# Attention with an added bias on one core: scores kept in PSUM across heads, and more exponentials on VectorE

## The chip, the core and the metric

The kernel runs on one core of a Trainium2 chip. The core has engines that run side by side and are ordered by semaphores: TensorE (PE in the profile; PEld is its loading of weights), VectorE (DVE), ScalarE (ACT) and GpSimd (POOL). The queues of SyncE (SP), ACT and POOL start transfers; those of POOL can convert f32 to bf16 on the way. Matmuls write into PSUM, a memory of eight banks of 512 f32 values for each of 128 partitions. SBUF is the larger memory that everything else lives in. The metric is the time of one execution on the device in microseconds, the median of several.

## The reference

For 4 batches with 8 heads each, a sequence of 1024 and a head dimension of 64, attention with a bias that all heads share:

```python
scores = scale * np.matmul(q, k.transpose(0, 1, 3, 2))   # scale = 1/8
scores = scores + bias                                    # (1, 1, 1024, 1024)
attn = np.exp(scores - scores_max) / (np.sum(np.exp(scores - scores_max), axis=-1, keepdims=True) + 1e-8)
return np.matmul(attn, v)
```

All inputs are f32, drawn with a standard deviation of 0.1. The kernel leaves out the subtraction of the maximum, since the scores are small, and gets the sum of a row's exponentials from a column of ones beside V.

## The kernel before

The 32 heads are taken as 16 pairs (`NP`). Scores are made transposed, keys on partitions and queries along the row, so that the exponentials can be the weights of the second product as they are. A *bank* is the unit of the scores: 128 keys (chunk `kc` of 8) by 512 queries (half `qh` of 2) of one head, one PSUM bank. There are 512 banks.

**Loads and transposes.** POOL loads K and Q of a pair with conversion to bf16 (`load_qk`, L75 to L80), three pairs ahead, and V two pairs ahead into `vall` (`load_v`, L82). TensorE transposes K and Q (`transpose_pe`, L86) into one of two single PSUM banks `xa` and `xb`; VectorE copies them out. K of both heads lies stacked on the partitions (head 0 on 0 to 63, head 1 on 64 to 127). Q is copied twice with a mask that zeroes the other head's half (L102), so that one matmul over 128 partitions gives the scores of one head.

**Scores and exponentials.** `s_fill` (L165) makes three banks with three matmuls of 512 columns (L172) in one of two PSUM tiles of three banks each (`ps_s`); `s_exp` (L178, L180) lets ScalarE exponentiate the three banks in one instruction into `E` in SBUF, as bf16. While ScalarE reads one tile, TensorE can fill the other.

**The bias.** For most banks exp(S + bias) is made as exp(S) times exp(bias): in the beginning the bias is transposed (`b_fill`, L220) and exponentiated once (`b_exp`, L230, L232) into `eb`, and VectorE multiplies every pair of banks by it (`mul_pair`, L235, two banks on L245 and L239, four on L242). For 64 banks (the chunks `kc` 6 and 7 of the second half of the queries) the bias is added in PSUM by one more matmul of 512 columns (L176, L193), and no product follows.

**Exponentials on VectorE.** Six of those 64 banks are never seen by ScalarE. VectorE turns the scores into fixed point (L201) and makes 2^x from integer and fraction with a polynomial in six further steps over two banks at a time (`d_steps`, L205, lines L212 to L217): two scalar operations and four that combine two operands.

**Second product.** `av_bank` (L261) multiplies the exponentials of a bank with V and the ones column, four matmuls of 65 columns each with its own weights (L269), summed over the chunks in `xa` or `xb`. The evacuation takes the reciprocal of the sum (L279), multiplies (L281), and SP's queue stores the result.

**The order of the work.** It is written out ahead by a planner (from L412): it keeps a clock for ScalarE, VectorE and TensorE, books each instruction with a fixed cost, and lets the engine that can start first emit its next one. TensorE prefers the fill of the next score tile (`pe_fill`, L470), and in the time that it is not needed takes a transpose (`pe_piece`, L496), a fill for VectorE's exponentials (`pe_d`, L553) or a product (`pe_av`, L635). VectorE takes what is ready first, by rank (`dve_pick`, L688). The engines then run these lists in order; only waits decide the actual times. The start (L324 to L410) is written by hand: the first half of the first pair is loaded by SP and ACT as f32, converted on VectorE and ScalarE, and dummy matmuls keep TensorE busy until then.

Of the kernel before, what the change touches and what calls it, by code (L numbers as in the profile page):

```python
# [16 lines left out]
def kernel(  # L17
# [11 lines left out]

# [7 lines left out]
    HQ = S // 2  # L40
    QC = NCH // 2
# [3 lines left out]
    vf = v.rearrange("b (g t) (p c) d -> (b g) p t c d", t=2, p=P)  # L45
    of = out.rearrange("b h (p c) d -> (b h) p c d", p=P)
    bf_ = bias.rearrange("a b (p c) k -> p (a b c) k", p=P)

    consts = ctx.enter_context(tc.tile_pool(name="consts", bufs=1))
    raw = ctx.enter_context(tc.tile_pool(name="raw", bufs=3))  # L50
    kvp = ctx.enter_context(tc.tile_pool(name="kvp", bufs=3))
    ep = ctx.enter_context(tc.tile_pool(name="ep", bufs=6))
    op = ctx.enter_context(tc.tile_pool(name="op", bufs=2))
    dp = ctx.enter_context(tc.tile_pool(name="dp", bufs=1))
    de = ctx.enter_context(tc.tile_pool(name="de", bufs=2))
    small = ctx.enter_context(tc.tile_pool(name="small", bufs=4))
    ps_s = ctx.enter_context(tc.tile_pool(name="ps_s", bufs=2, space=bass.MemoryType.PSUM))
    ps_x = ctx.enter_context(tc.tile_pool(name="ps_x", bufs=1, space=bass.MemoryType.PSUM))

    ident = consts.tile([P, P], BF)  # L60
    warm = consts.tile([P, 1], F32)
    btraw = consts.tile([P, NCH, S], BF)
    eb = consts.tile([P, 2, NCH, HQ], BF)
    braw = consts.tile([P, 2, HQ], BF)
    mask = consts.tile([P, 2, HQ], BF)
    vall = consts.tile([P, 2 * NP, NCH, D1], BF)

    k0f = consts.tile([P, 2, QC, D], F32)
    q0f = [consts.tile([P, QC, D], F32, name=f"q0f{t}") for t in range(2)]
    zeros = consts.tile([P, P], BF)  # L70

    raws = {}
    trs = {}

    def load_qk(pr):  # L75
        qr = raw.tile([P, 2, NCH, D], BF, name="qr")
        kr = raw.tile([P, 2, NCH, D], BF, name="kr")
        nc.gpsimd.dma_start(out=kr.rearrange("p t c d -> p t (c d)"), in_=kf[pr])  # L78
        nc.gpsimd.dma_start(out=qr.rearrange("p t c d -> p t (c d)"), in_=qf[pr])  # L79
        raws[pr] = (qr, kr)  # L80

    def load_v(pr):  # L82
        for t in range(2):
            nc.gpsimd.dma_start(out=vall[:, 2 * pr + t, :, :D], in_=vf[pr, :, t])  # L84

    def transpose_pe(pr, which, c0, n, tag):  # L86

        src = raws[pr][which]
        px = ps_x.tile([P, n, P], BF, tag=tag, name="px")
        for c in range(n):  # L90
            for t in range(2):
                nc.tensor.transpose(px[t * D:(t + 1) * D, c, :], src[:, t, c0 + c, :], ident[:])  # L92
        if (pr, which) not in trs:
            trs[(pr, which)] = (kvp.tile([P, NCH, P], BF, name="kT") if which else
                                kvp.tile([P, 2, NCH * P], BF, name="qT"))
        dst = trs[(pr, which)]

        def copy():
            if which == 0:

                m = n // QC
                nc.vector.tensor_tensor(  # L102
                    dst[:, :, c0 * P:(c0 + n) * P].rearrange("p t (m q) -> p t m q", m=m),
                    px.rearrange("p (m c) q -> p m (c q)", m=m).unsqueeze(1).to_broadcast([P, 2, m, HQ]),
                    mask.unsqueeze(2).to_broadcast([P, 2, m, HQ]), op=ALU.mult)
            else:
                nc.vector.tensor_copy(dst[:, c0:c0 + n, :], px[:])  # L107
        return copy


    NE = NCH - 2
    DPR = (3, 7, 11)
    banks = [(0, h, 0, kc) for kc in range(NCH) for h in range(2)]

    def mix(early, late, singles):
        while early or late:
            if late and (singles(len(banks), len(early) + len(late)) or not early):
                banks.append(late.pop(0))
            else:
                banks.extend(early[:2])  # L120
                del early[:2]

    for pr in range(NP):
        early = [(pr, h, 1, kc) for kc in range(NE) for h in range(2)]
        late = [(pr, h, 1, kc) for kc in range(NE, NCH - (pr in DPR)) for h in range(2)]
        if pr == NP - 1:
            early = [(pr, h, 1, kc) for h in range(2) for kc in range(NE)]
            late = [(pr, h, 1, kc) for h in range(2) for kc in range(NE, NCH)]
        if pr == 0:
            early += [(1, h, 0, kc) for kc in range(NCH) for h in range(2)]  # L130
            mix(early, late, lambda b, left: b % 3 == 2 and b > 36)
        else:
            if pr > 1:
                banks += [(pr, h, 0, kc) for kc in range(NCH) for h in range(2)]
            mix(early, late, lambda b, left: b % 3 == 2 and (pr < NP - 1 or left > 8))
    NB = len(banks)

    dgroups = []
    for pr in DPR:
        dgroups.append((pr, [len(banks), len(banks) + 1]))  # L140
        banks += [(pr, h, 1, NCH - 1) for h in range(2)]
# [5 lines left out]
    for b in range(len(banks)):  # L147
        units.setdefault(banks[b][:3], []).append(b)
# [112 lines left out]
    def av_bank(b, tag):  # L261
# [9 lines left out]
        if not last:  # L271
            return None
# [522 lines left out]
```

## Time and profile before

Three runs gave 246.46, 246.47 and 246.8 us; the median is 246.47 us.

| What | before |
|---|---|
| profiled execution (span) | 246.5 us |
| ACT busy | 236.7 us, 96%, 181 instructions |
| PE busy | 229.9 us, 93%, 3154 matmuls |
| DVE busy | 219.2 us, 89%, 366 instructions |
| POOL busy | 55.3 us, 22% |
| exponentials of scores (L180) | 170 instructions, 227.9 us |
| exp(bias) (L232) | 4 instructions, 6.7 us |
| products with exp(bias) (L242, L245) | 158 instructions, 136.4 us |
| matmuls for the scores (L172) | 454 in the trace, 134.9 us |
| DMA | 23.80 MB moved, mean 97 GB/s |

How to read it: the busy time of an engine is the time in which at least one of its instructions runs. Instructions in a row overlap in part, so the time of one (its mean in ns) can be longer than the distance from one start to the next; where many follow each other, the distance counts. For matmuls the ends are modelled, so that PE looks busier than it is. In the line of slices each digit is the busy share, in tenths, of one fortieth of the span. In the groups, "idle before" is the time for which the engine sat idle ahead of these instructions and what it waited for. A few matmul records are missing from the trace (454 of the 506 matmuls of L172 are in it).

### The profile page before, as it was taken

Reading aid. Unit: us, or ns where it says so; the run is one execution under the profiler, and the core shown is the slowest. Engines: PE = TensorE matmul, PEld = TensorE weight load, DVE = VectorE, ACT = ScalarE, POOL = GpSimd, SP = SyncE. Lnnn points to the kernel's source line nnn. Section 1 sums busy time; section 2 is a strip of 40 time slices with the busy share of each in tenths; the row PEclk is TensorE's granted clock in tenths of the full one; section 3 lists DMA queues with packets and bytes.
Section 4 is the critical chain, followed back from the end, with each engine's and each line's share of the span. In section 5 each row is a group of like instructions: output and inputs, shape, how many; then the busy total and the mean of one; then the engine's idle time right before and its main releaser. Section 6 shows DMA issues by size and latency. Waiting matters only on the chain.

```text
span 246.5 us, 7234 instructions
## 1 busy us (share of the span) xinstructions
PE 229.9 (93%) x3154; PEld 144.8 (59%) x3207; DVE 219.2 (89%) x366; ACT 236.7 (96%) x181; POOL 55.3 (22%) x76
## 2 busy tenths in 40 slices
PE   8667999999999999999988999999998999999993
PEld 3244656665566656666654665666664566766653
DVE  2417799998999999999999999999999999999994
ACT  5599999999999999999999999999999999999993
POOL 7654333501441304140134000601500000000000
PEclk9799999999999999999999999999999999999999
DMA  5999995995689479492394920792911020202022
GB/s 113 179 197 193 192 131 102 148 84 122 65 123 160 51 122 121 107 116 80 56 127 91 82 88 25 114 122 75 140 45 45 1 88 4 86 1 88 35 77 65
DMA packets 48752, 23.80 MB, mean 97 GB/s; under 512 B 34512, under 2 KB 44624, under 8 KB 48720
## 3 DMA queue, kind: packets, MB, share of 16 engines
q0 software_dynamic: 42560, 14.42, 53.6%
q1 hardware_dynamic: 5872, 8.72, 9.8%
q8 instruction: 25, 0.41, 0.7%
q10 hardware_dynamic: 288, 0.20, 0.3%
q14 instruction: 7, 0.06, 0.1%
HBM read 29.36 MB, written 8.39 MB: 153 GB/s over the span
## 4 chain that ended last, share of the span: by engine, by line
ACT 45%; PE 44%; DVE 4%; DMA 2%; issue 2%; POOL 1%; ACTq 0%; POOLq 0%
ACT E L180 42%; PE ps L172 24%; PE po L269 13%; PE px L92 3%; PE ps L176 3%; ACT eb L232 3%; DMA kr<-in_k_dram 2%; DVE qT L102 1%; DVE E L242 1%; DVE E L239 1%; PE pd L192 1%; PE pd L193 1%; DVE oall L281 1%; DVE db L215 0%; DVE dy L201 0%
## 5 line engine op out<-in xcount | busy, mean ns | idle before, releaser
L180 ACT ACTIVATE E<-ps 128x1536 bf16<-128x1536 f32 (+1 forms) x170 | 227.9, 1525 | 2.8 <-PE ps L172 2.7
L172 PE MATMUL ps<-qT,kT 128*128 128x512 bf16 x454 | 134.9, 382 | 8.2 <-ACT E L180 3.3
L269 PEld LDWEIGHTS <-E 128*128 128x128 bf16 x1992 | 78.9, 98 | 34.1 <-DVE E L242 2.5
L269 PE MATMUL po<-vall,E 128*128 128x65 bf16 x1992 | 84.8, 194 | 0.8 <-DVE E L245 0.3
L242 DVE TENSOR_TENSOR E<-E,eb 128x2048 bf16<-128x2048 bf16 x60 | 72.4, 1217 | 0.0
L245 DVE TENSOR_TENSOR E<-E,eb 128x1024 bf16<-128x1024 bf16 x98 | 64.0, 683 | 4.2 <-ACT eb L232 4.0
L172 PEld LDWEIGHTS <-kT 128*128 128x128 bf16 x506 | 44.9, 97 | 36.6 <-issue 10.2
L84 POOL DMA_DIRECT2D vall<-in_v_dram x32 | 28.7, 902 | 7.1 <-DMA btraw<-in_bias_dram 3.5
L281 DVE TENSOR_TENSOR oall<-po,rs 128x256 f32<-128x256 f32 x63 | 26.7, 425 | 2.2
L78 POOL DMA_DIRECT2D kr<-in_k_dram x15 | 10.5, 699 | 64.5 <-PE px L92 62.4
L102 DVE TENSOR_TENSOR qT<-px,mask 128x2048 bf16<-128x2048 bf16 (+1 forms) x17 | 19.2, 1127 | 5.6 <-PE px L92 5.4
L79 POOL DMA_DIRECT2D qr<-in_q_dram x15 | 10.7, 716 | 48.2 <-PE px L92 47.2
L176 PE MATMUL ps<-braw,ident 128*128 128x512 bf16 x57 | 21.4, 378 | 0.1
L279 DVE RECIPROCAL rs<-po 128x4 f32<-128x4 f32 x63 | 11.2, 178 | 3.3 <-PE po L269 2.5
L107 DVE COPY kT<-px 128x1024 bf16<-128x1024 bf16 (+1 forms) x16 | 10.4, 652 | 0.8 <-PE px L92 0.8
L92 PEld LDWEIGHTS <-qr 128*64 128x64 bf16 x248 | 7.5, 109 | 5.4 <-issue 5.1
L92 PEld LDWEIGHTS <-kr 128*64 128x64 bf16 x240 | 7.2, 109 | 5.0 <-issue 4.7
L92 PE MATMUL px<-ident,qr 128*64 128x128 bf16 x248 | 10.2, 222 | 0.0
L92 PE MATMUL px<-ident,kr 128*64 128x128 bf16 x240 | 9.7, 222 | 0.0
L176 PEld LDWEIGHTS <-ident 128*128 128x128 bf16 x58 | 5.6, 97 | 6.9
L232 ACT ACTIVATE eb<-pb 128x2048 bf16<-128x2048 bf16 (+1 forms) x4 | 6.7, 1676 | 0.0
L226 PEld LDWEIGHTS <-btraw 128*128 128x128 bf16 x56 | 4.0, 146 | 2.0 <-issue 1.6
(59 smaller groups left out, 65.7 us busy)
## 6 DMA issues: line engine op xcount, KB each, us to landing
out_dram<-oall SPq DMA_DIRECT2D x28, 256.0 KB, 2.0
vall<-in_v_dram POOLq DMA_DIRECT2D x32, 128.0 KB, 5.5
kr<-in_k_dram POOLq DMA_DIRECT2D x15, 256.0 KB, 4.3
qr<-in_q_dram POOLq DMA_DIRECT2D x15, 256.0 KB, 4.7
btraw<-in_bias_dram POOLq DMA_DIRECT2D x4, 512.0 KB, 8.7
out_dram<-oall SPq DMA_DIRECT2D x7, 128.0 KB, 1.8
k0f<-in_k_dram SPq DMA_DIRECT2D x2, 128.0 KB, 3.0
q0f<-in_q_dram ACTq DMA_DIRECT2D x1, 128.0 KB, 2.6
```

The lines of the kernel that those rows point to most:

```text
L84: nc.gpsimd.dma_start(out=vall[:, 2 * pr + t, :, :D], in_=vf[pr, :, t])
L92: nc.tensor.transpose(px[t * D:(t + 1) * D, c, :], src[:, t, c0 + c, :], ident[:])
L102: nc.vector.tensor_tensor(dst[:, :, c0 * P:(c0 + n) * P].rearrange("p t (m q) -> p t m q", m=m), px.rearrange("p (m c) q -> p m (c q)", m= ...
L172: nc.tensor.matmul(ps[:, j, :], kT[:, kc, :], qT[:, h, qh * HQ:(qh + 1) * HQ], start=True, stop=b not in late_bias)
L176: nc.tensor.matmul(ps[:, j, :], ident[:], braw[:, late_bias[b], :], start=False, stop=True)
L180: nc.scalar.activation(e_at(slots[g][0], n), open_ps.pop(("S", g))[:, :n, :], ACTF.Exp, scale=scale)
L232: nc.scalar.activation(eb[:, qh, :n, c0 * P:(c0 + 2) * P], open_ps.pop(("B", qh, c0))[:, :n].rearrange("p k c q -> p k (c q)"), ACTF.Exp)
L242: nc.vector.tensor_tensor(e, e, eb[:, qh, kc:kc + 2, :].unsqueeze(2).to_broadcast([P, 2, 2, HQ]), op=ALU.mult)
L245: nc.vector.tensor_tensor(e, e, eb[:, qh, kc:kc + 1, :].to_broadcast([P, n, HQ]), op=ALU.mult)
L269: nc.tensor.matmul(acc[:, i, :], e[:, 0, i * P:(i + 1) * P], vall[:, 2 * pr + h, kc, :], start=(first and i == 0), stop=last, skip_group_c ...
L279: nc.vector.reciprocal(rs[:], acc[:, :, D:D1])
L281: nc.vector.tensor_tensor(oall[:, c0:c0 + QC, :], acc[:, :, :D], rs[:].to_broadcast([P, QC, D]), op=ALU.mult)
```

## The change

The change rewrites how the scores are made and ordered.

*Running scores.* The queries are split into three passes of chunks of 128: A takes chunks 6 and 7, B 3 to 5, C 0 to 2. Six PSUM banks, `XY`, two tiles of three, hold the scores plus the bias for one pass, the even half-step in one and the odd in the other (pass A uses two banks of each). At the start of a pass (a *restart*) the bias is transposed into PSUM by matmuls of 128 columns, with the bias as weights and 8 times the identity moving, and the first head's scores are added. For each further head the tile is not made anew: one matmul over 128 partitions adds this head's scores and takes away the last head's. For head 1 of a pair the operands are `KA` (both heads stacked) and `QA` (the first half negated); for head 0 they are `KB` and `QB`, in which the second half belongs to the pair before. ScalarE's exp reads the tile and leaves it as it is. The order is: pairs 0 and 1 in the passes A, B, C; pairs 2 to 7 in C, B, A; pairs 8 to 15 in A, B, C. That makes 96 steps (a pass, a pair, a head) of two half-steps, and seven restarts.

*No exp(bias).* `eb`, `mul_pair`, the mask and the separate handling of the late chunks go.

*Operands.* K and Q of up to nine pairs are kept. VectorE copies K out of PSUM, copies Q out with a sign for each partition, and makes -Q in SBUF. Since `KB` and `QB` have halves of neighbouring pairs, four copies from SBUF to SBUF for each pair go through SP's queue. V is loaded in one DMA for a pair into a dense tile, and VectorE copies it beside the ones column.

*VectorE's exponentials.* Chunks of two banks (the last bank of both half-steps of a head 0) are marked while the order is planned, whenever VectorE's booked load is under a bound and fewer than two chunks are open; 40 banks come out. Their scores are read from the running tile in PSUM (`d_fixed`), so the tile's next fill waits for this as well as for the exp. The six further steps use the same scratch for all chunks.

*Products.* A unit is a pair in a pass: both heads are summed in one PSUM bank (`xa` or `xb`), and evacuated and stored together. The products are taken in the order of the units; within a unit, whichever bank is ready first. E is one ring of 44 banks.

*Start.* The first exp needs K of head 0, chunks 6 and 7 of Q and column chunk 6 of the bias, all loaded as f32 by SP and ACT and converted; the rest of the bias comes on POOL's queue.

```diff
-                m = n // QC
-                nc.vector.tensor_tensor(
-                    dst[:, :, c0 * P:(c0 + n) * P].rearrange("p t (m q) -> p t m q", m=m),
-                    px.rearrange("p (m c) q -> p m (c q)", m=m).unsqueeze(1).to_broadcast([P, 2, m, HQ]),
-                    mask.unsqueeze(2).to_broadcast([P, 2, m, HQ]), op=ALU.mult)
...
+    def v_copy(pr):
+        nc.vector.tensor_copy(VV[:, pr % RP, :, :D], vst.pop(pr)[:])
...
+    def k_out(pr, px):
+        nc.vector.tensor_copy(KA[:, pr % RP, :], px.rearrange("p c q -> p (c q)"))
+        if pr > 1:
+            nc.sync.dma_start(out=KB[:D, pr % RP, :], in_=KA[:D, pr % RP, :])
+        if pr + 1 < NP:
+            nc.sync.dma_start(out=KB[D:, (pr + 1) % RP, :], in_=KA[D:, pr % RP, :])
+
+    def q_out(pr, px):
+        nc.vector.tensor_scalar(QA[:, pr % RP, :], px.rearrange("p c q -> p (c q)"), sgn[:, :1], None, op0=ALU.mult)
+
+    def q_neg(pr, c0=0):
+        qn = qnp.tile([P, NCH * P], BF, name="qn")
+        nc.vector.tensor_scalar(qn[:], QA[:, pr % RP, :], -1.0, None, op0=ALU.mult)
+        nc.sync.dma_start(out=QB[:D, pr % RP, c0:], in_=qn[:D, c0:])
+        if pr + 1 < NP:
+            nc.sync.dma_start(out=QB[D:, (pr + 1) % RP, :], in_=qn[D:, :])
...
+        if restart:
...
+                    nc.tensor.matmul(ps_[:, cc:cc + P],
+                                     btraw[:, c + j, :].rearrange("p (kp kc) -> p kc kp", kc=NCH)[:, kc, :],
+                                     ident8[:], start=cc // 512 not in seen, stop=False, skip_group_check=True)
...
+        for kc, c, n, col in pcs:
+            kcol, qcol = slice(kc * P, (kc + 1) * P), slice(c * P, (c + n) * P)
+            o = ps_[:, col:col + n * P]
+            if restart:
+                lhsT, rhs = KA[:D, r, kcol], QB[:D, r, qcol]
+            elif h == 1:
+                lhsT, rhs = KA[:, r, kcol], QA[:, r, qcol]
             else:
...
+                lhsT, rhs = KB[:, r, kcol], QB[:, r, qcol]
+            nc.tensor.matmul(o, lhsT, rhs, start=False, stop=True, skip_group_check=True)
...
+    def s_exp(s, n, pos):
+        e_pos[s] = pos
+        nc.scalar.activation(E[:, pos * 512:(pos + n) * 512], XY[s % 2][:, :n * 512], ACTF.Exp, scale=scale)
...
+    def d_fixed(ch, j, s, b):
+        y = ys[ch % 2].bitcast(I32)
+        nc.vector.tensor_scalar(y[:, j * 512:(j + 1) * 512], XY[s % 2][:, b * 512:(b + 1) * 512],
+                                scale * LOG2E * 65536.0, 127.0 * 65536.0, op0=ALU.mult, op1=ALU.add)
...
+            (690, lambda: v_.tensor_scalar(sf, lo, G / 65536.0, None, op0=ALU.mult)),
+            (690, lambda: v_.tensor_scalar(sp, hi, 0.0, 128.0, op0=ALU.max, op1=ALU.mult)),
+            (1217, lambda: v_.scalar_tensor_tensor(y, sf, U1, sf, op0=ALU.add, op1=ALU.mult)),
+            (1217, lambda: v_.scalar_tensor_tensor(sb, sf, U2, sf, op0=ALU.add, op1=ALU.mult)),
+            (1217, lambda: v_.scalar_tensor_tensor(sb, sb, V2, sp.bitcast(BF), op0=ALU.add, op1=ALU.mult)),
+            (1217, lambda: v_.scalar_tensor_tensor(e[:], y, V1, sb, op0=ALU.add, op1=ALU.mult)),
...
-    def mul_pair(b, n=2):
...
+        nc.vector.reciprocal(rs[:], acc[:, :, :, D:D1])
+        nc.vector.tensor_tensor(ob[:], acc[:, :, :, :D], rs[:].to_broadcast([P, 2, W, D]), op=ALU.mult)
+        nc.sync.dma_start(out=of[pr][:, :, c0 * D:(c0 + W) * D], in_=ob.rearrange("p t c d -> p t (c d)"))
...
+        nc.sync.dma_start(out=k0f[:, :NCH * D], in_=kf[0][:, 0])
+        nc.scalar.dma_start(out=c6f, in_=bf_[:, 6, :])
+        nc.sync.dma_start(out=q0f.rearrange("p (t x) -> p t x", t=2), in_=qf[0][:, :, 6 * D:])
+        nc.sync.dma_start(out=k0f[:, NCH * D:], in_=kf[0][:, 1])
+        nc.scalar.dma_start(out=c7f, in_=bf_[:, 7, :])
...
+        load_qk(1)
+        nc.gpsimd.dma_start(out=qr0[:, :, :6, :].rearrange("p t c d -> p t (c d)"), in_=qf[0][:, :, :6 * D])
+        load_v(0)
+        nc.gpsimd.dma_start(out=btraw[:, 3:6, :], in_=bf_[:, 3:6, :])
+        load_v(1)
+        nc.gpsimd.dma_start(out=btraw[:, :3, :], in_=bf_[:, :3, :])
+        load_qk(2)
...
+            ready = max(act_end[s - 2], fix_end.get(s - 2, 0), o) + SEM
...
+                if h == 0 and s % 2 == 0:
+                    if d_load - t < DLIM and len(open_ch) < 2 and s >= DMIN and s < NS - DTAIL:
...
+                        d_load = max(d_load, t) + 7800
...
+        DLIM, DMIN, DTAIL, DMAL, RING, PSL, URG = 3500, 8, 10, 2600, 12, 180, 6
```

## Prediction

> **What bounds the kernel now.** I read the profile's page first (busy shares, slices), then the groups of instructions with their shapes apart, then the waits, then the timeline of single engines. The profiled execution takes 246.5 us, the median of the runs shown is 246.47 us, so the sum can be made against the span.
>
> The page's busy shares and its forty slices:
>
> ```profile
> PE 229.9 (93%) x3154; PEld 144.8 (59%) x3207; DVE 219.2 (89%) x366; ACT 236.7 (96%) x181; POOL 55.3 (22%) x76
> ...
> ACT  5599999999999999999999999999999999999993
> ```
>
> ACT is at 9 from the third slice to the last but one. From 9.71 us (first full exp) to 241.73 us (end of the last) the stage view gives it 232.02 us busy of 232.02. The waits say the same: of the few times that ACT waited for a matmul, nearly all is one wait of 2.6 us in the start.
>
> ```profile
> ACT E L180 <- PE ps L172: 2.7, 2, 2.6
> PE ps L172 <- ACT E L180: 3.3, 10, 0.5
> ```
>
> So the time is 9.7 us of start + 232.0 us of ScalarE + 4.8 us of tail. VectorE and TensorE have little room, but nothing of theirs ends last. The durations I need, from the groups by shape (mean ns is a single instruction's latency):
>
> ```profile
> L180 ACT ACTIVATE E<-ps 128x1536 bf16<-128x1536 f32 x167 | 225.4, 1536 | 2.6 <-PE ps L172 2.6
> L232 ACT ACTIVATE eb<-pb 128x2048 bf16<-128x2048 bf16 x2 | 3.8, 1890 | 0.0
> L281 DVE TENSOR_TENSOR oall<-po,rs 128x256 f32<-128x256 f32 x63 | 26.7, 425 | 2.2
> L107 DVE COPY kT<-px 128x1024 bf16<-128x1024 bf16 x14 | 9.6, 685 | 0.0
> L201 DVE TENSOR_SCALAR dy<-pd 128x512 int32<-128x512 f32 x6 | 4.1, 686 | 0.7 <-PE pd L193 0.6
> L217 DVE SCALAR_TENSOR_TENSOR de<-dy,db 128x1024 bf16<-128x1024 f32 x3 | 3.7, 1219 | 0.0
> L212 DVE TENSOR_SCALAR df<-dy 128x1024 f32<-128x1024 uint16 x3 | 2.1, 685 | 0.0
> ```
>
> What a row costs in a full stream is the distance between starts. The chain has the large activations one after the other: 1.34 to 1.35 us for three banks, 1.77 us for 2048 elements. Two sizes give 0.06 us + 0.427 us per 512 elements. VectorE's timeline gives its steps: independent instructions start 0.60 us apart where one lasts 0.68, while a multiply that needs the reciprocal starts 0.03 us after that has ended.
>
> ```profile
> 103.03 0.68 DVE L245 TENSOR_TENSOR E<-E,eb 128x1024 bf16<-128x1024 bf16 x1
> 103.69 0.18 DVE L279 RECIPROCAL rs<-po 128x4 f32<-128x4 f32 x1
> 103.90 0.42 DVE L281 TENSOR_TENSOR oall<-po,rs 128x256 f32<-128x256 f32 x1
> 104.25 1.28 DVE L245 TENSOR_TENSOR E<-E,eb 128x1024 bf16<-128x1024 bf16 x2
> ```
>
> **ScalarE.** The change splits the 512 banks of scores into 64 half-steps of two banks (pass A) and 128 of three (B, C), and 40 of the banks go to VectorE. Instructions: 64 x 0.916 + 128 x 1.343 - 40 x 0.427 = 58.6 + 171.9 - 17.1 = 213.4 us. Before, by the same rule: 167 x 1.343 + 0.9 + 6.2 for the four exp(bias) = 231.4. ScalarE loses 18 us; what follows decides how much of that is kept.
>
> **Start.** Before, ACT streams from 9.71 us with three banks (1.3 us) already done. Now the first exp needs half of pair 0's K (256 KB), a column of the bias (512 KB), a bit of Q (128 KB), a cast (L212's 0.69) and 24 matmuls of 128 columns. The old start's 128 KB loads took 3.0 us to land; the page's slices move 113 to 197 GB/s. The 0.9 MB needed, with the 0.77 MB queued beside it, lands between 5 us (only its own bytes, twice 190 GB/s since cast loads read two bytes for each one counted) and 10 us (all of it at 190). With cast and matmuls (x6 of 512 took 2.74 us just then, half speed) the first exp lies between 7.5 and 13 us. I take 9.9, the middle of the landing. Pass B needs a bias of 1.5 MB on POOL's queue behind K, Q and V of two pairs, by 17.2 us (9.9 + 8 x 0.916); with all ahead of it that is 5.1 MB read, 3.4 MB written. At twice 190 GB/s of reading it is there at 15, at the page's written bytes (0.7 MB in the first slice of 6.2 us, 1.1 in each later one) at 21: a loss of 0 to 4 us, 2 taken.
>
> **VectorE.** It loses the 98 + 60 multiplies by exp(bias) (136 us of rows) and the masked Q copies (19), and gets:
> - 20 chunks of two banks: two L201, L212 and L213 at 0.68, four like L217. All overlapped: 4 x 0.60 + 4 x 1.13 = 6.9 us; all dependent (each duration + 0.03): 7.8. Most steps here read their predecessor, so 7.45: 149 us.
> - 48 evacuations of both heads: reciprocal 0.21 and a multiply of 384 or 256 (by L281 and L217 about 1.03 ns an element: 557 or 425 long, 0.47 or 0.34 apart): 32 x 0.69 + 16 x 0.55 = 31.
> - per pair a K and a Q copy out of PSUM like L107 (0.65 each), a negation of Q and a copy of V inside SBUF. No row has these two: the planner books 0.34 each; bounds are L107's 0.69 for the negation, 1.2 (L217's full rate) for V with its stride of 65, and 0.29 (L373's cast of 256) for both. I take 0.40 and 0.45, nearer to what is booked, since L107's source is PSUM: 16 x 2.15 = 34.
> With 2 us of start: 216 us. This is as much as before (219.2), but it has to fit: the first chunk is marked at half-step 8 (17.2 us), the last at half-step 180, whose successors are 12 exps (15 us), and the units behind the last chunk need 4.4 us of products and 3.5 of evacuation and store. So some 211 us must lie between 17.2 us and 8 us before the end: a span of 236 us if VectorE never idles.
>
> **TensorE.** The QK columns are the same 262,144 (0.65 us for three 512s: 111 us), now in 1280 instructions instead of 512. Nearest row for 128 columns with their own weights is L226:
>
> ```profile
> 13.89 1.13 PE L226 MATMUL pb<-ident,btraw 128*128 128x128 bf16 x16 [0.54 <-ACT E L180]
> ```
>
> (1.13 - 0.22) / 15 = 60 ns, 6 above a quarter of 217: at most 8 us more; I take 4: 115. The 63 bias matmuls of 512 columns (L176 and L193, 13.7) and 64 bias transposes (3.8) go, 152 restart matmuls come (9.1). Products (20 in 0.61: 62.5) and transposes (16 in 0.57: 18.2) stay. Sum 205 against 209: no longer than before, but in a shorter span, so it is 92% filled.
>
> **The wait that is added.** A score bank may be refilled only when the exp and, for a chunk, VectorE's read of it (L201) are over, since the sums stay in PSUM. What queues behind it: the fill on TensorE, then ACT's exp after next. A fill ends about 0.6 us before its exp starts (1.343 - 0.67 - 0.08). VectorE's running instruction leaves 0 to 1.13 us. In passes B and C the read is over at +0.7 (mean) against the exp's end at +0.92: no stall mostly, 0.35 at the worst, 0.25 taken. In pass A (exps of 0.49, fills of 0.46) the refill comes 0.6 to 2.1 us late per chunk; 1.0 taken. With 13 and 7 chunks: 10 us (bounds 4 and 19). Restarts add 12 bias matmuls to a fill (0.67 + 0.70 against 1.343), 0.4 x 6 = 2, partly hidden by the same stalls. The copies K and Q to the other half (four 128 KB DMAs a pair on SP's queue, which waits for VectorE in order; old 256 KB stores landed in 2.0 us) run a pair or more ahead of use: nothing; without that cover, 2 us at a pass's first pairs.
>
> **A rule against it.** POOL's DMA issues took 0.70 to 0.90 us each in the trace. The Trainium skill's "SBUF — State Buffer" (Who interferes with whom) says that VectorE's copies and scalar ops in two-port modes lock GpSimd out for the whole instruction, descriptor writing included. By the row the new single-source ops cost POOL nothing; by the rule each of about 45 issues could wait a further 0.7 us, spread over queues that run ahead, so the sum is the same.
>
> **Sum.** ACT's path: 9.9 + 213.4 + 2 + 10 (restarts inside it) + tail 5.0 (4.8, with a longer last multiply and store, without the split of the last unit) = 240; VectorE's: 236. They are nearly the same load, and the chunks' late reads are the same waits seen twice, so I take 238.
>
> **The rivals.**
> 1. Stalls hide better: pass A's reads find VectorE free and TensorE's slack takes the rest. 9.9 + 213.4 + 5 + 2 to 4 = 230 to 232. For it: ACT lost 2.8 us in the whole old run. Against: VectorE's 216 us and its idle ends.
> 2. VectorE becomes the bound, slower than before. Its products come in unit order, so a late chunk holds all later products, and the 44 banks of E are 44 x 0.427 = 18.8 us of exps. Chunks at 7.8 (+7), the pair copies at their upper bounds (0.72 + 0.72 + 0.72 + 1.2 per pair, +20): 236 + 27 = 263 at most; slower than before from +10.5 us, that is from 227 us of VectorE work. For it: the chain's steps depend on each other; V's odd stride. Against: one-source rows of 1024 all take 0.68.
> 3. Reads hold the PSUM banks at their worst: 19 us instead of 10 gives 247; it decides from 0.95 us a chunk. Against: the read is put ahead of other VectorE work.
> 4. Weight loads of the smaller matmuls show (97 ns each, 768 more): + 74 us, well over 300. L226's 60 ns and the products' 30 ns speak against it.
>
> **How the numbers follow.** Forecast (233 to 246, likeliest part 234 to 243) 0.60; rival 1 0.13; rivals 2, 3 and 4 together 0.24 (0.15, 0.08, 0.01); within 0.2% (0.5 us, about what this kernel's runs, 246.46 to 246.8, can tell apart) 0.03. Faster is forecast and rival 1, 0.73. The range leaves out a part of rival 1 and the far end of rival 2: 230 to 252.
>
> **What the profile after would show.** ACT: 192 exps, 213 us busy, and waits for the fills of some 10 us, most of it in the two long A passes (right) or under 4 (rival 1). VectorE at 9 in nearly every slice, a chunk's four large steps 1.14 to 1.25 us apart; V's copy near 0.4 us. TensorE's granted clock at 1 and 8 matmuls of a pass A fill in 0.46 us. The prediction is wrong if the first exp starts past 12 us, if TensorE waits for late chunks with ACT idle behind a full E, or if V's copy takes 1 us.

## The result and the profile after

The change makes the kernel slower. It takes 286.68 us (median of four runs, 285.87 to 289.08) against 246.52 us for the kernel before, run beside it: a ratio of 1.165, with an interval of 1.160 to 1.170. 238 was forecast, and the range ended at 252. The profiled execution took 286.06 us, with a span of 284.3. A run more than 1.5% above the fastest of its kernel counts as slow and is left out of the ratios: experiments 1 and 4 have one such run each, and their times below are the medians of the other three (276.43 and 282.45 us; with it 277.09, which later expectations call 277.1, and 283.31).

The page of the changed kernel: busy shares and slices, the two groups of exponentials, and VectorE's read of scores from PSUM (columns: line, engine, operation, tiles and count | busy us, mean ns of one | idle before, and its main releaser).

```profile
PE 236.3 (83%) x3999; PEld 194.7 (68%) x3999; DVE 213.4 (75%) x337; ACT 226.0 (80%) x197; POOL 35.9 (13%) x55
...
ACT  2477899864898899888988755357998999999893
...
DMA  7999999999940236812989951001221100011112
...
L188 ACT ACTIVATE E<-sx 128x1024 bf16<-128x1024 f32 (+2 forms) x96 | 117.5, 1224 | 29.7 <-PE sx L182 20.5
L188 ACT ACTIVATE E<-sy 128x1024 bf16<-128x1024 f32 (+2 forms) x96 | 117.5, 1224 | 18.1 <-PE po L248 9.9
...
L199 DVE TENSOR_SCALAR scr<-sx 128x512 int32<-128x512 f32 x20 | 13.8, 689 | 18.1 <-ACT E L188 17.3
```

Before, ACT stood at 9 from the third slice to the last but one. Now fewer than half of the slices reach 9, and slices 24 to 27 hold 5, 5, 3 and 5. No engine is full: VectorE idles for 71 us, and yet its reads of `sx` (L199) have 18 us of idle ahead of them, nearly all of it waiting for ScalarE. Who waits for whom (engine, line, what it waited for: us in total, times, longest):

```profile
DVE scr L199 <- ACT E L188: 30.2, 26, 4.4
ACT E L188 <- PE sx L182: 20.5, 22, 3.8
ACT E L188 <- PE po L248: 15.0, 14, 1.9
PE sy L182 <- DVE scr L199: 6.8, 12, 0.9
PE sx L182 <- DVE scr L199: 5.3, 10, 0.8
ACT E L188 <- DVE scr L199: 4.9, 8, 1.4
```

Three kinds of wait are new or far longer. VectorE's read waits for an exp, although the exp reads other banks. ScalarE waits for fills, some of which wait for that read or for a copy of K or Q. And ScalarE waits for products (`po`, L248) that are to empty the ring E.

The sum of the prediction can be laid beside ScalarE's own timeline, exp by exp:

| Term | sum of the prediction | measured |
|---|---|---|
| first exp starts | 9.9 | 10.63 |
| 192 exps at the distances of a full stream | 213.4 | 213.4 (the same 192 sizes; the distances too: 0.92 us at 13.06, 1.33 at 61.83) |
| idle shown after the first exp | 2 + 10 | 44.6, in 58 pauses |
| what is left over | 0 | 11.1 |
| from the last exp's end to the end | 5.0 | 4.5 |
| sum | 240 | 284.2 |

The left-over term is the overlap that each pause loses (an exp of two banks lasts 1.02 us but starts 0.92 after its predecessor in a stream: 58 x 0.1 = 6) and waits too short to be listed. So ScalarE's work is what was forecast, and the error is idleness. By stage the 44.6 us are: 4.0 up to 22.3 us, 11.6 from there to 80, 5.7 to 155, 18.1 from 155 to 195, 5.3 to the end (these five add to 44.7 by rounding).

The stages' busy times (stretch and its length, then busy us and instructions of PE, PEld, DVE, ACT, POOL; granted TensorE clock, DMA share, GB/s):

```profile
40.00:80.00 40.00, 31.09 (x488) 23.41 (x485) 29.43 (x49) 30.84 (x25) 12.31 (x18) 0.96 1.10 215
...
155.00:195.00 40.00, 29.97 (x491) 26.46 (x492) 22.62 (x39) 21.91 (x24) 0.00 (x0) 0.83 0.35 78
195.00:277.00 82.00, 71.82 (x1224) 58.78 (x1224) 70.31 (x102) 76.15 (x61) 0.00 (x0) 1.00 0.15 43
```

From 40 to 80 us the sixteen DMA engines are full. They were nearly so before, in the same stretch, and ScalarE never idled, so nearly full DMA engines alone do not make it wait; the GB/s, 117 then, are 215 now:

```profile
40.00:80.00 40.00, 39.33 (x572) 25.11 (x582) 38.35 (x61) 40.00 (x31) 13.07 (x16) 1.00 0.90 117
```

From 155 to 195 us every engine has idle time: ScalarE 18 of 40 us, VectorE 17, TensorE 10.

### The profile page after: what moved, and what is told of

It is laid out like the page before. It is cut to its first block, busy times and chain, and to the rows that moved or that the text cites. A ratio compares the mean times of both kernels' runs of the same rounds, so it can differ in the third digit from the quotient of the medians.

```text
span 284.3 us, 9122 instructions
## 1 busy us (share of the span) xinstructions
PE 236.3 (83%) x3999; PEld 194.7 (68%) x3999; DVE 213.4 (75%) x337; ACT 226.0 (80%) x197; POOL 35.9 (13%) x55
## 2 busy tenths in 40 slices
DMA packets 31575, 31.94 MB, mean 112 GB/s; under 512 B 2544, under 2 KB 27184, under 8 KB 31536
## 4 chain that ended last, share of the span: by engine, by line
ACT 32%; PE 30%; DVE 19%; DMA 8%; issue 8%; ACTq 1%; SPq 0%; DVEq 0%
ACT E L188 32%; PE sx L182 9%; PE sy L182 8%; DVE scr L199 7%; PE po L248 7%; DMA QB<-qn 3%; DMA KB<-KA 3%; PE sx L169 2%; DMA scr<-in_q_dram 2%; DVE e L215 2%; PE px L137 2%; PE sy L169 2%; DVE ob L259 1%; DVE scr L214 1%; DVE scr L210 1%
## 5 line engine op out<-in xcount | busy, mean ns | idle before, releaser
L188 ACT ACTIVATE E<-sx 128x1024 bf16<-128x1024 f32 (+2 forms) x96 | 117.5, 1224 | 29.7 <-PE sx L182 20.5
L188 ACT ACTIVATE E<-sy 128x1024 bf16<-128x1024 f32 (+2 forms) x96 | 117.5, 1224 | 18.1 <-PE po L248 9.9
L182 PEld LDWEIGHTS <-KA 128*128 128x128 bf16 (+1 forms) x732 | 56.5, 99 | 38.1 <-issue 28.1
L248 PE MATMUL po<-VV,E 128*128 128x65 bf16 x1888 | 79.5, 195 | 0.4 <-ACT E L188 0.4
L248 PEld LDWEIGHTS <-E 128*128 128x128 bf16 x1888 | 73.5, 99 | 5.3 <-ACT E L188 0.5
L182 PEld LDWEIGHTS <-KB 128*128 128x128 bf16 x548 | 41.8, 99 | 24.5 <-issue 15.5
L182 PE MATMUL sy<-QA,KA 128*128 128x128 bf16 (+1 forms) x320 | 36.7, 255 | 11.8 <-DVE scr L199 6.8
L182 PE MATMUL sx<-QA,KA 128*128 128x128 bf16 (+1 forms) x320 | 36.7, 255 | 10.4 <-DVE scr L199 5.3
L182 PE MATMUL sx<-QB,KB 128*128 128x128 bf16 (+2 forms) x274 | 31.6, 256 | 9.1 <-ACT E L188 3.6
L182 PE MATMUL sy<-QB,KB 128*128 128x128 bf16 (+2 forms) x274 | 31.6, 256 | 5.6 <-ACT E L188 5.4
L199 DVE TENSOR_SCALAR scr<-sx 128x512 int32<-128x512 f32 x20 | 13.8, 689 | 18.1 <-ACT E L188 17.3
L212 DVE SCALAR_TENSOR_TENSOR scr<-scr 128x1024 f32<-128x1024 f32 x20 | 24.4, 1220 | 0.3
L214 DVE SCALAR_TENSOR_TENSOR scr<-scr 128x1024 f32<-128x1024 f32 x20 | 24.4, 1219 | 0.3
L213 DVE SCALAR_TENSOR_TENSOR scr<-scr 128x1024 f32<-128x1024 f32 x20 | 24.3, 1217 | 0.0
L199 DVE TENSOR_SCALAR scr<-sy 128x512 int32<-128x512 f32 x20 | 13.8, 690 | 13.0 <-ACT E L188 12.9
L128 POOL DMA_DIRECT2D vs<-in_v_dram x16 | 11.4, 715 | 58.8 <-DVE VV L132 50.1
## 6 DMA issues: line engine op xcount, KB each, us to landing
btraw<-in_bias_dram POOLq DMA_DIRECT2D x2, 768.0 KB, 14.5
```

What stands on the lines that cost most here:

```text
L128: nc.gpsimd.dma_start(out=vs.rearrange("p (t c) d -> p t (c d)", t=2), in_=vf[pr])
L182: nc.tensor.matmul(o, lhsT, rhs, start=False, stop=True, skip_group_check=True)
L188: nc.scalar.activation(E[:, pos * 512:(pos + n) * 512], XY[s % 2][:, :n * 512], ACTF.Exp, scale=scale)
L199: nc.vector.tensor_scalar(y[:, j * 512:(j + 1) * 512], XY[s % 2][:, b * 512:(b + 1) * 512], scale * LOG2E * 65536.0, 127.0 * 65536.0, op0= ...
L212: (1217, lambda: v_.scalar_tensor_tensor(y, sf, U1, sf, op0=ALU.add, op1=ALU.mult)),
L213: (1217, lambda: v_.scalar_tensor_tensor(sb, sf, U2, sf, op0=ALU.add, op1=ALU.mult)),
```

## The experiments

The letters in the expectations name theories. A: VectorE's read and ScalarE's exp of the same half-step shut each other out, since both banks lie in one PSUM tile, so that a marked half-step costs fill, exp, read, one after the other. C and D: the operands come late, since K, Q and V of all pairs of a group are needed in its first pass. The others are told where they fall.

What led to A was a stretch of the changed kernel's timeline (start, us, engine and line, tiles, [idle before, releaser]; other lines left out):

```profile
23.93 1.02 ACT L188 ACTIVATE E<-sy 128x1024 bf16<-128x1024 f32 x1 [0.63 <-PE sy L182]
...
24.98 0.69 DVE L199 TENSOR_SCALAR scr<-sy 128x512 int32<-128x512 f32 x1 [0.97 <-ACT E L188]
...
25.73 0.81 PE L182 MATMUL sy<-QA,KA 128*128 128x384 bf16 x6 [0.33 <-DVE scr L199]
26.58 1.45 ACT L188 ACTIVATE E<-sy 128x1536 bf16<-128x1536 f32 x1 [0.21 <-PE sy L182]
```

The exp of banks 0 and 1 of `sy` ends at 24.95, the read of bank 2 starts at 24.98, the refill after the read's end at 25.67, the next exp of `sy` after that: of these steps on one tile none overlaps another. So it is throughout: none of the 40 reads runs beside an exp of its tile. What led to C was a copy:

```profile
66.87 1.44 PE L182 MATMUL sx<-QB,KB 128*128 128x384 bf16 x6 [2.17 <-DMA KB<-KA]
...
68.40 1.45 ACT L188 ACTIVATE E<-sx 128x1536 bf16<-128x1536 f32 x1 [3.79 <-PE sx L182]
```

**1. No exponentials on VectorE.** ScalarE does all 512 banks.

```diff
-        DLIM, DMIN, DTAIL, DMAL, RING, PSL, URG = 3500, 8, 10, 2600, 12, 180, 6
+        DLIM, DMIN, DTAIL, DMAL, RING, PSL, URG = 3500, 9999, 10, 2600, 12, 180, 6
```

> No chunk is marked, so VectorE exponentiates nothing and ScalarE all 512 banks; all else of the change stays. Theory A (the added time comes from the chunks: VectorE's read of a score bank and the exp of the same tile exclude each other, and products that wait for a late chunk fill the ring E): ScalarE streams after the start, so 12.2 us (start as in the trace) + 64 x 0.916 + 128 x 1.343 = 230.5 + 5 us tail + 1.9 us outside the span = 250 us, to 256 with the waits at restarts and for the copied K and Q. Rival B (the running sums themselves are slow: more and smaller matmuls, restarts, copies through the DMA queue): the waits stay, 46 us of them, and 17 us of exps come back: 290 to 303 us. Rival C (the start and the copied K and Q alone, about 4 and 7 us in the trace): 256 to 262 us.

Measured: 276.43 us, ratio 1.118 (1.111 to 1.126). No theory had it: A and C were too low, B too high. ScalarE's work is 230.5 us here (17.1 more), and the kernel is still 10.3 us faster, so the exponentials on VectorE cost more than they save. But of the 46.3 us for which ScalarE idled ahead of exps 26.4 stay without them, with VectorE busy for 27% of the span: shutting-out can't be the only cause.

**2 and 3. VectorE's bank in its own PSUM tile, with a control.** The control cuts the exps into two instructions over the same tiles (one stays where the last bank is VectorE's); the experiment has the same two instructions, in the same order, with the last bank in a tile of its own.

```diff
+    def xy(s, a, b):
+        return XY[s % 2][:, a:b]
...
-        nc.scalar.activation(E[:, pos * 512:(pos + n) * 512], XY[s % 2][:, :n * 512], ACTF.Exp, scale=scale)
+        lo = 2 if nbanks(steps[s // 2][0]) == 3 else 1
+        for a, b in ((0, lo), (lo, n)):
+            if b > a:
+                nc.scalar.activation(E[:, (pos + a) * 512:(pos + b) * 512], xy(s, a * 512, b * 512), ACTF.Exp, scale=scale)
```

That is the control. The experiment has, besides:

```diff
-    XY = [ps.tile([P, 3 * 512], F32, tag=t, name=t) for t in ("sx", "sy")]
+    XY = [ps.tile([P, 2 * 512], F32, tag=t, name=t) for t in ("sx", "sy")]
+    XL = [ps.tile([P, 512], F32, tag=t, name=t) for t in ("lx", "ly")]
...
+    def xy(s, a, b):
+        d = 1024 if nbanks(steps[s // 2][0]) == 3 else 512
+        return XL[s % 2][:, a - d:b - d] if a >= d else XY[s % 2][:, a:b]
```

> Control of the next run: the order is kept, but each exp is cut in two instructions (banks 0 and 1, then bank 2; in pass A one bank each), over the same two PSUM tiles. 152 more instructions at 0.06 us make 9 us of ScalarE, part of it in time that ScalarE waits anyway. Theory A and rivals alike: 287 to 297 us.

> As the control, but the last bank of each half-step, which VectorE may read, is a PSUM tile of its own, so that VectorE's read waits for the fill alone and not for the exp of the other banks. Theory A: the waits between the read and the exp (30 us of VectorE's, and 17 us of ScalarE's and TensorE's for the read) go, and with them part of the later lateness: 12 to 30 us less than the control. Rival B or C: within 3 us of the control.

Measured: the control 289.14 us, the own tile 268.94 us (ratios 1.173, 1.169 to 1.176, and 1.092, 1.089 to 1.095). The control's waits, then the one that is left of them with the own tile, from 22 us on:

```profile
DVE scr L205 <- ACT E L194: 31.2, 29, 2.8
...
PE sy L182 <- DVE scr L205: 6.8, 12, 0.9
...
PE sx L182 <- DVE scr L205: 5.3, 11, 0.8
```

```profile
DVE scr L206 <- ACT E L195: 0.9, 4, 0.3
```

In the own-tile kernel the two engines do read at once, at 38 of the 40 reads (the control: at none):

```profile
28.03 1.08 ACT L195 ACTIVATE E<-sy 128x1024 bf16<-128x1024 f32 x1
...
28.24 0.68 DVE L206 TENSOR_SCALAR scr<-ly 128x512 int32<-128x512 f32 x1
```

So theory A holds, and the tile of its own is worth 20.2 us. The wait is the program's own: two readers of one tile are put in order, whichever banks they touch. Not all of the 20.2 need be that order, since the refills have become freer as well: at 94 of the 152 half-steps without a chunk TensorE now starts to refill the first tile before the exp of the last bank is over, by 0.3 us on the mean. No run parts the two. The Trainium skill's "PSUM — Partial Sum Buffer" (PSUM bank collisions raise a hardware error) asks for such an order only between accesses to the same bank, reads against reads included, and says that different banks may be read together. The last two lines agree with the second part; no run here shows the first.

**4. A planner that books more for copies.** The planner is told that a copy takes 5.2 us instead of 2.6.

```diff
-        DLIM, DMIN, DTAIL, DMAL, RING, PSL, URG = 3500, 8, 10, 2600, 12, 180, 6
+        DLIM, DMIN, DTAIL, DMAL, RING, PSL, URG = 3500, 8, 10, 5200, 12, 180, 6
```

> The planner books 5.2 us in place of 2.6 for a copy of K or Q to land (the trace has 4.6 and 4.9). Theory A: the waits for these copies go (about 5 us in the trace), the rest stays: 279 to 287 us, unless the new order happens to be better or worse for the chunks. Rival C: 10 us or more faster, 270 to 277 us.

Measured: 282.45 us, ratio 1.143 (1.136 to 1.151), against 1.160 to 1.170 of the change. A gain of some 4 us: a wrongly booked copy is a small part.

**5 and 6. Few loads.** K and Q of pairs 0 to 2 and V of pairs 0 and 1 are loaded; the later pairs use K and Q of pairs 1 and 2 and this V again, so the result is another one, and the loads' waiting and their bytes go together. In 5 this is done without exponentials on VectorE, in 6 with them in their own tile.

```diff
     def load_qk(pr):
+        if pr > 2:
+            raws[pr, 1], raws[pr, 0] = raws[1 + pr % 2, 1], raws[1 + pr % 2, 0]
+            return
...
     def load_v(pr):
+        if pr > 1:
+            vst[pr] = vst0[pr % 2]
+            return
```

> The kernel without chunks, and K and Q are loaded only for pairs 0 to 2, V only for pairs 0 and 1; the later pairs transpose and use these again, so that the output is another one and 20 MB of reading are left out. All else, copies of K and Q through SP's queue included, is as in the run without chunks (277.1 us). Theory D (the transfers are the bound in the passes that first use a pair: the DMA engines are full from 7 to 78 us and from 142 to 165 us, and ScalarE waits there): the waits for operands go, 16 us of the 27 that this run lost against its plan; start and restarts stay: 258 to 264 us. Rival E (the operand chain of transposes and VectorE copies in the order of TensorE is what is late, whatever the transfers do): 273 to 278 us.

> The kernel with a PSUM tile of its own for VectorE's bank (268.9 us), with the same loads left out. Theory D: 10 to 16 us less, 253 to 259 us. Rival E: 266 to 270 us.

Measured: 261.96 us (14.5 less than experiment 1) and 258.86 us (10.1 less than experiment 3). The page of experiment 5 shows where: from the fifth slice on the DMA engines stand at 7 or less, mostly at 2 or less, and ACT is at 9 from the seventh on, but for one 8 and the last.

```profile
ACT  3346989999999999999999999899999999999993
...
DMA  7998022564632321101113765211110110210111
```

The copies themselves change most. Their rows (DMA issues: KB each, median us from issue to landing) in the changed kernel, in experiment 1 and in experiment 5:

```profile
KB<-KA SPq DMA_DIRECT2D x28, 128.0 KB, 4.6
QB<-qn SPq DMA_DIRECT2D x28, 128.0 KB, 4.9
```

```profile
KB<-KA SPq DMA_DIRECT2D x28, 128.0 KB, 5.2
QB<-qn SPq DMA_DIRECT2D x28, 128.0 KB, 5.5
```

```profile
KB<-KA SPq DMA_DIRECT2D x28, 128.0 KB, 2.4
QB<-qn SPq DMA_DIRECT2D x28, 128.0 KB, 2.5
```

The same 128 KB landed in less than half the time of experiment 1. The transfers cost 10 to 15 us; what of that is late loads and what slowed copies, these two runs do not part.

**7. The longer booking without exponentials on VectorE.** The edit of 4 on experiment 1.

```diff
-        DLIM, DMIN, DTAIL, DMAL, RING, PSL, URG = 3500, 9999, 10, 2600, 12, 180, 6
+        DLIM, DMIN, DTAIL, DMAL, RING, PSL, URG = 3500, 9999, 10, 5200, 12, 180, 6
```

> The kernel without chunks, with 5.2 us in place of 2.6 booked for a copy of K or Q to land. Theory D: a later booked landing doesn't move the bytes any sooner, 273 to 279 us. Rival F (only the booked latency was wrong, and TensorE's order waits for copies that it takes too early): 262 to 268 us.

Measured: 273.82 us, ratio 1.110 (1.108 to 1.113); experiment 1's interval was 1.111 to 1.126, so the two are not clearly apart. Booking the copies' true landing does not give the 14.5 us back, which leaves the transfers themselves.

**8. The planner knows of the order.** The same tiles as the change; VectorE reads first, and ScalarE's exp is booked after the read.

```diff
+            if i in mark and i not in fix_end:
+                return None
-            return max(t_act, fill_end[i] + SEM), act_cost(i), i, pos
+            return max(t_act, max(fill_end[i], fix_end.get(i, 0)) + SEM), act_cost(i), i, pos
```

> The changed kernel, but the planner knows that the read and the exp of a tile exclude each other: VectorE reads its bank first, and the exp is booked behind it. Theory A: the exclusion costs by itself, whoever goes first; the planner books the last exp 21 us later than in the changed kernel (254.7 in place of 234.0 us), and the lateness for start and operands comes on top: 272 to 282 us. Rival G (what costs is the wrong plan, engines waiting in order for one another, and not the exclusion): 262 to 270 us.

Measured: 275.18 us, ratio 1.116 (1.110 to 1.122). The planner then marked 46 banks instead of 40. The wait has turned round: now the exp waits for the read.

```profile
ACT E L188 <- DVE scr L199: 25.7, 37, 1.6
```

The order costs by itself, known or not: the own-tile kernel is 6.2 us faster, although ScalarE has more to do there. The change is 11.5 us slower than this, and only 2.5 of them are ScalarE's work (210.9 us here). That the rest is the price of lists planned for a course that did not come about is argued: the order of the readers, the marks and all lists changed together.

**9. Transfers spread out.** Experiment 1 with groups of 2, 4, 5 and 5 pairs instead of 2, 6 and 8, and other orders of the passes; the same bytes, but nine restarts instead of seven.

```diff
-    groups = [(range(0, 2), "ABC"), (range(2, 8), "CBA"), (range(8, NP), "ABC")]
+    groups = [(range(0, 2), "ABC"), (range(2, 6), "CAB"), (range(6, 11), "BAC"), (range(11, NP), "CAB")]
```

> The kernel without chunks (277.1 us), with the pairs in four groups (2, 4, 5, 5) in place of three (2, 6, 8), in the pass orders ABC, CAB, BAC, CAB. New pairs are used first in a long pass, and fewer of them one after the other, while all bytes are moved as before; nine restarts in place of seven. Theory D (the transfers are the bound where the pairs of a group are first used): much of the 15 us that went with the loads comes back, 264 to 271 us. Rival H (the total of the bytes counts, wherever it is moved): 274 to 279 us.

Measured: 268.77 us, ratio 1.091 (1.085 to 1.098), 7.7 us less than experiment 1. The edit also spreads the transposes and the copies by VectorE, and it parts the two A passes that follow each other in the change, so not all of the 7.7 need be the transfers'.

**10. Own tile, spread groups, and marks on the even half-steps only.** The marks move from both half-steps of head 0 to the even half-steps of both heads, so that only `sx` is cut and fewer extra activations are needed.

```diff
-    XY = [ps.tile([P, 3 * 512], F32, tag=t, name=t) for t in ("sx", "sy")]
+    XY = [ps.tile([P, n * 512], F32, tag=t, name=t) for t, n in (("sx", 2), ("sy", 3))]
+    XL = ps.tile([P, 512], F32, tag="lx", name="lx")
...
-    groups = [(range(0, 2), "ABC"), (range(2, 8), "CBA"), (range(8, NP), "ABC")]
+    groups = [(range(0, 2), "ABC"), (range(2, 6), "CAB"), (range(6, 11), "BAC"), (range(11, NP), "CAB")]
...
-                            mark[s + j] = (nch, j)
...
+                            mark[s + 2 * j] = (nch, j)
```

> 40 banks on VectorE again: each chunk is now the last bank of the even half-step of both heads, and only the tile of even half-steps has that bank as a PSUM tile of its own, so that the exp of the odd ones stays one instruction (62 more instructions at 0.06 us, 4 us). Pairs in the groups 2, 4, 5, 5. Theories A and D together: the kernel with own tiles (268.9 us) less 5 us of cut exps less 6 to 10 us of waits for operands, 253 to 259 us. If the exclusion or the transfers were not the causes: 265 us or more.

Measured: 273.44 us, ratio 1.109 (1.105 to 1.114). A miss: it is slower than either edit was expected to leave it, and experiment 12 takes it apart. Its waits have a new entry, VectorE's read waiting for the fill:

```profile
DVE scr L208 <- PE lx L189: 15.8, 16, 4.4
```

**11. The start without the bias.** Experiment 5 with the bias columns 6 and 7 set to zero instead of loaded, so that 1 MB less is read ahead of the first exp; VectorE's casts of these columns go with it, and the result is another one.

```diff
-        nc.scalar.dma_start(out=c6f, in_=bf_[:, 6, :])
...
-        nc.scalar.dma_start(out=c7f, in_=bf_[:, 7, :])
+        nc.vector.memset(btraw[:, 6:, :], 0.0)
...
-        nc.vector.tensor_copy(btraw[:, 6, :], c6f)
...
-        nc.vector.tensor_copy(btraw[:, 7, :], c7f)
```

> The kernel without chunks and with few loads (262.0 us), and the two columns of the bias that pass A begins with are zeros written by VectorE in place of 1 MB loaded and cast: those columns' bias is left out, and so is 1 MB beside the first K and Q. If the start is long for its bytes (Q landed at 6.9 us, the cast bias was there at 8.7, the first exp came at 10.9): first exp at 7.5 to 9 us and 258.5 to 260.5 us in all. If it is long for the chain of small steps on slow TensorE: first exp at 10 us or later, and 261 to 263 us.

Measured: 256.48 us, ratio 1.041 (1.038 to 1.044), 5.5 us less than experiment 5, where 1.5 to 3.5 was expected. The first exp and the first one of pass B (`sx`, three banks), in experiment 5:

```profile
10.88 1.03 ACT L196 ACTIVATE E<-sx 128x1024 bf16<-128x1024 f32 x1 [1.66 <-PE sx L190]
...
25.69 1.45 ACT L196 ACTIVATE E<-sx 128x1536 bf16<-128x1536 f32 x1 [0.84 <-PE sx L190]
```

And without those loads:

```profile
7.62 1.02 ACT L196 ACTIVATE E<-sx 128x1024 bf16<-128x1024 f32 x1 [0.94 <-PE sx L190]
...
18.84 1.45 ACT L196 ACTIVATE E<-sx 128x1536 bf16<-128x1536 f32 x1 [0.82 <-PE sx L190]
```

The first exp moves by 3.3 us and pass B by 6.9: the pauses inside the first eight exps get shorter too (later work gives a little back). A first exp in time is not yet a start in time. The loads and the casts went together, so the 5.5 us are the price of both.

**12. Own tile and spread groups, with the old marks.** Experiment 3 with the groups of 9, and so with its nine restarts (the expectation's "seven" is a slip).

```diff
-    groups = [(range(0, 2), "ABC"), (range(2, 8), "CBA"), (range(8, NP), "ABC")]
+    groups = [(range(0, 2), "ABC"), (range(2, 6), "CAB"), (range(6, 11), "BAC"), (range(11, NP), "CAB")]
```

> The kernel in which VectorE's bank of every half-step has its own PSUM tile (268.94 us), with one change: the seven restarts lie between groups of 2, 4, 5 and 5 pairs (passes ABC, CAB, BAC, CAB), as in the kernel without VectorE's exponentials that this brought from 277.09 to 268.77 us. The whole computation is there, with the same bytes. It takes apart the two edits of the kernel that ended at 273.44 us. Theory D (transfers cost here too, 10.1 us by the run with few loads, and spreading them gives back about half, as it did without the chunks: 8.3 of 15.1 us): 260 to 265 us, and then it was the marks on other half-steps that cost that kernel its gain. Theory G (with the chunks, TensorE's and VectorE's lists in their fixed order wait on each other, and a transfer that comes earlier only moves the wait): 267 to 275 us. Between 265 and 267 neither.

Measured: 261.73 us, ratio 1.059 (1.053 to 1.065), within theory D's 260 to 265: the groups give 7.2 us here, and experiment 10's loss came with its other marks and the odd half-steps left uncut in one tile (11.7 us, although ScalarE has 6 us less to do there). How these cost that is only argued: one tile serves every second half-step, VectorE takes its list in order, and a read that waits for its fill holds all that is behind it.

The page of experiment 12 and two of its stages:

```profile
ACT  3358999787378999999999999999999999989993
...
DMA  7999999999872644789982291442212112101121
```

```profile
22.00:80.00 58.00, 49.15 (x770) 39.04 (x770) 44.01 (x70) 46.34 (x65) 14.63 (x20) 0.91 1.00 189
...
155.00:195.00 40.00, 38.54 (x655) 31.12 (x654) 37.24 (x58) 39.66 (x57) 0.00 (x0) 1.00 0.32 79
```

The hole from 155 to 195 us is gone: ScalarE is busy for 39.66 of 40 us, and after 80 us it has 2.4 us of listed idle in all. What is left is the start, 11.4 us of idle from 22 to 80 us, where the DMA engines are still full, and the price of cutting the exps: by the distances, ScalarE's work is 222.9 us instead of 213.4. No version beat the kernel before.

## Why the prediction was wrong

**What was right.** ScalarE's count and prices: 213.4 us of work. VectorE's 216 us: 213.4 measured, with V's copy at 0.424 us (taken 0.45), the negation at 0.440 (0.40), and a chunk's large steps, where they follow each other, mostly 1.25 us apart (1.13 to 1.26). TensorE's matmuls of 128 columns: eight in 0.61 us, 56 ns apart by (0.61 - 0.22) / 7, against the row's 60; rival 4 is out. POOL's issues: 0.72 and 0.74 us for K and Q, 0.70 and 0.72 before, so the rule on the shared port showed no price here. The tail: 4.5 for 5.0. TensorE's sum, 4 us under the one before, did not come true: its busy time by the page rose from 229.9 to 236.3 us, part of it at a lowered clock.

**"The wait that is added" failed.** It was taken as 10 us, with bounds of 4 and 19, from a model in which VectorE's read runs beside the exp ("the read is over at +0.7 (mean) against the exp's end at +0.92"). The traces show that the two never run side by side while they share a tile, and experiments 2 and 3 that a tile for each is worth 20.2 us, beyond the upper bound. (Its split was off as well: 4 of the 20 chunks fell in pass A, not 7, which at its own prices makes 8 us.) What the prediction had computed was the wait for VectorE to become free; the wait that came was for ScalarE to be done. Rival 3 had the right wait, the PSUM bank held too long, but its price rested on the same model. The wait could have been bounded: exp, then read, then fill, then exp on one tile is 1.02 + 0.69 + 0.81 us in the stretch shown above, and the rows of before had like durations (0.69 for the read L201).

**The copies "nothing" failed, and the loads with them.** The cover named was that the copies "run a pair or more ahead of use", at 2.0 us each, which was the old stores' landing. They landed in 4.6 and 4.9 us, beside loads that took 7.7 us for K (4.3 before), where a group's first pass now needs K, Q and V of all its pairs. 31.94 MB were moved, 23.80 before; these 56 copies are 7.3 of the difference. Transfers cost 14.5 us by experiments 1 and 5, 10.1 by 3 and 6. The prediction counted the instructions that each moved step issues, but not the bytes per microsecond of a pass.

**The start was a size.** The first exp came at 10.63 us, taken 9.9. But pass B began at 22.27 instead of 19.2 (9.9 + 8 x 0.916 + 2), 3 us later, through pauses within the first eight exps.

**VectorE as the bound (rival 2): the wait came, the bound did not.** The sign named for it, ScalarE idle behind a full E, is there: 15.0 us, 13.4 of it between 155 and 195 us.

```profile
170.20 1.02 ACT L188 ACTIVATE E<-sx 128x1024 bf16<-128x1024 f32 x1 [1.69 <-PE po L248]
...
179.98 1.02 ACT L188 ACTIVATE E<-sy 128x1024 bf16<-128x1024 f32 x1 [1.82 <-PE po L248]
```

But VectorE is idle for 17 of those 40 us: it was not short of time. The wait does come with the chunks, as rival 2 has it; without them (experiment 1) this is left:

```profile
ACT E L188 <- PE po L248: 1.1, 1, 1.1
```

That lists in a fixed order hold one another there is the reading that fits, but no run takes it by itself, and TensorE's clock was low there too (0.83). With the own tile the wait for products falls from 15.0 to 8.8 us, with few loads as well to 7.9, and with the groups of experiment 12 ScalarE has no listed wait in that stretch.

**How far the loss is accounted for.** Against the forecast of 238 us 48.7 are missing. The own tile is worth 20.2 by experiments 2 and 3, of which the forecast's sum already held 10 as the added wait; the transfers are 10.1 once it is there (3 and 6). The start's bias loads are 5.5 by experiment 11, of which the forecast held part, with its first exp at 9.9 and 2 us of pauses. If these add up, 23 us or more are left. ScalarE's own idleness is nearer to closed: after the first exp the listed idle is 44.6 us in the change, 12 in the forecast's sum, and 15.2 in experiment 6, with own tile and few loads, whose exps are 9.5 us longer by their cuts. Spreading the groups took a further 7.2 us from experiment 3, and with them the idle where the first pass of eight pairs meets the pass before it; how the rest divides between the ring, the fixed order and the pair's own transposes and copies was not separated.

## What to carry to other kernels

Before two engines are counted as reading side by side, look at which tile each reads, since a program's waits go by tile: give the second reader its own tile, and bound the wait by the whole cycle of fill, first reader, second reader. When a loop order is turned so that one pass needs the operands of many units, add up the bytes per microsecond of that pass, its copies included, before any transfer is called hidden. And sums of busy times can come true, as ScalarE's and VectorE's did here, while the time is a sixth longer: the idleness needs bounds of its own.

## What the runs showed of the hardware

- TensorE's clock was low in a stage where it waited often, but the busy share alone does not tell when. In the stage from 155 to 195 us, where TensorE was busy for 30 of 40 us, the mean granted clock was 0.83, and eight matmuls of 128 columns at 173.18 us took 1.01 us, where they took 0.61 at 171.28. In experiment 12, with TensorE busy for 38.5 of 40 us there, the clock was 1.00. But it was 1.00 as well in the changed kernel's first 40 us, with 32.6 us busy, and 0.89 in experiment 1 from 155 to 195 us, with 37.0 busy. No run takes this cost by itself.
- A copy of 128 KB within SBUF landed in 2.4 us with few loads beside it (experiment 5), in 4.6 to 4.9 in the changed kernel, and in 5.8 to 6.0 in experiment 9, which was faster than its parent all the same (5.2 and 5.5 there). So the landing time alone does not say what a copy costs; that it depends on how far ahead the copy is issued is likely, and not shown.
